# Attention roots, rotations and query splits with an operand in PSUM, keys rotated ahead of their root, and a minimum collected with its sign

## The chip, the cores and the metric

The kernel runs on one core of a Trainium2 chip. Its time is device time in microseconds (us) of one execution; three executions of the kernel before took 2225.22, 2225.4 and 2231.34 us. The engines are TensorE (PE, with its weight loads shown apart as PEld), VectorE (DVE), ScalarE (ACT), GpSimd (POOL) and SyncE (SP), which issues the transfers. [...]

## The reference

Four layers run over 256 latent tokens with a prefix of 256 context tokens, each layer followed by a gated MLP. Layers 0 and 3 are windowed attention with sink logits (16 query heads and 4 key heads of 64), layer 1 is multi-head latent attention (MLA), layer 2 a gated recurrence. What the change touches is the root of each head's norm, the rotation and the softmax:

```python
def rmsnorm(x, gain):
    xf = x.astype(jnp.float32)
    y = xf * lax.rsqrt(jnp.mean(xf * xf, axis=-1, keepdims=True) + EPS)
    return (y * gain.astype(jnp.float32)).astype(x.dtype)

def attend(q, k, v, mask=None, sink=None):
    s = jnp.einsum("bqhgd,bkhd->bhgqk", q, k, preferred_element_type=jnp.float32) * (q.shape[-1] ** -0.5)
    ...
    m = jnp.max(s, axis=-1)
    ...
        m = jnp.maximum(m, sk)
    p = jnp.exp(s - m[..., None])
    denom = jnp.sum(p, axis=-1)
```

Queries and keys are normalised per head (`rmsnorm`), then latent ones are rotated: each half of a head is multiplied with cosines, and its swapped copy with sines is added. A norm's factor is one number for each token and head, so it commutes with the rotation. MLA does the same on heads of 96, of which 32 are rotated, and norms two low-rank projections besides.

## The kernel before

The 512 tokens lie in four blocks b of 128 (0 and 1 context, 2 and 3 latent). Every weight is used as a sum of two halves for precision: SP loads `raw`, ACT rounds it to `whi` (L222), POOL subtracts to get `wlo` (L226, in pieces of 128x256), and each product is three matmuls (L235, L236, L237). A framework places every engine's instructions in one static order, and reorders attention work around the projections. PSUM has four pools of two banks each (128x512): mm, fl, mo and tp. A bank is free for its next product once its last reader is done.

An inverse root has no instruction of its own on this path: `mean_rsqrt` and `rsqrt` (L272 to L287) work it out on DVE from an integer shift, a magic constant and three Newton steps, 12 instructions on tiles of 128x4, 128x8 or 128x16, all of them in SBUF (`rs_v`, `rs_i`, `rs_y`, `rs_t`):

```python
for _ in range(steps):
    nc.vector.tensor_tensor(t, y, y, op=ALU.mult)
    nc.vector.scalar_tensor_tensor(t, t, -0.5, v, op0=ALU.mult, op1=ALU.mult)
    nc.vector.scalar_tensor_tensor(y, t, 1.5, y, op0=ALU.add, op1=ALU.mult)
```

There are 30 such roots: 24 on 128x8 (12 for queries of the windowed layers, 12 in MLA's loop), 4 on 128x16 and 2 on 128x4. The layers' own norms have another, `psum_rsqrt` (L289 to L300), in which each instruction has an operand in PSUM; it runs 15 times.

Windowed attention (`swa`, L576 on) goes as follows. *Keys*, L634 to L658: ACT copies a block of the keys out of PSUM (`kraw`, L638), copies the values, squares `kraw` (L641); DVE sums by head (L642). After the fourth block one root of 128x16 follows, then for each block a multiply by it (L650), the rotation (L617, or L574, L621 and L622 for latent blocks), ACT's doubling copy (L655), and PE's transposes (L660), which are split into `k_hi` and `k_lo` (L269, L270). *Queries*, `q_post`, L663 to L691: ACT squares the PSUM bank, DVE sums (L674) and rotates into `qr` in SBUF; each half is split (ACT L681, DVE L682), transposed (L685) and copied; the root becomes `rqs`, a factor of the scores (L691). *Cores*, L699 to L755: the scores (L696, L697), for latent blocks one instruction that scales, masks and takes the maximum (L723), a sign change (L726), the exponential (L727), the division, transposes (L745) and the product with the values (L751). Products of the next head group, `proj(2)`, go into the fl banks between them. Layer 3 handles latent queries only.

MLA (`mla`, L783 on) runs in head groups. For each block of the next group `kv_mm` makes keys and values, `q_mm` makes queries in an fl bank (L899 to L913, rotation in L908 and L909), one root of 128x8 serves both, then `kv_put` multiplies the keys by it (L883, L884, into `kn`) and transposes them (L888), and `q_scale` (L920) makes `rqs`.

## Time and profile before

| | before |
|---|---|
| runs (us) | 2225.4, 2231.34, 2225.22 |
| profiled execution: its own time | 2225.85 us |
| its span | 2224.0 us |
| PE busy, share of the span | 2122.6 us, 95% |
| DVE busy | 1549.0 us, 70% |
| ACT busy | 1037.4 us, 47% |
| POOL busy | 1050.3 us, 47% |
| mean granted clock | 0.983 |

The span runs from the first to the last instruction; 1.85 us lie around it. Busy shares are averages over stages with different limits. The chain of waits is followed back from the last instruction. A timeline row gives start, duration, engine, line, output and inputs, shape and count, and in brackets the idle time before it and what released it. Matmuls are pipelined, so their durations overlap.

### The profile page before, as it was taken

The page shows a single profiled execution, that of the slowest core. Times are in us where ns is not written, and L with a number is a line of the kernel's source. Part 1 is how long each engine was busy: PE and PEld are TensorE (multiplying, and loading weights), DVE is VectorE, ACT ScalarE, POOL GpSimd, SP SyncE. Part 2 cuts the span into 40 slices and gives each one's busy share as a digit, 9 for nine tenths or more (in the row PEclk, how much of TensorE's full clock was granted, in tenths as well). Part 3 has the DMA queues.
Part 4 walks back from the last instruction along what each step waited for, and adds up shares of the span by engine and source line. Part 5 has one row for each costly group of instructions (what it writes and reads, how often), then busy time and mean ns, then how long its engine had stood idle before and what let it go on. Part 6 is the DMA issues. An engine that isn't in the chain of part 4 may idle for free.

```text
span 2224.0 us, 32888 instructions
## 1 busy us (share of the span) xinstructions
PE 2122.6 (95%) x12084; PEld 1764.6 (79%) x12084; DVE 1549.0 (70%) x3341; ACT 1037.4 (47%) x1860; POOL 1050.3 (47%) x760
## 2 busy tenths in 40 slices
PE   6999999999999999999999999889999999898999
PEld 4666888888888666878888887678888888678999
DVE  4677779777776886687888677857954456785333
ACT  4467553232346775532233376824332324675544
POOL 3331255544544113455455457654544444526887
PEclk9999999999999999999999999999999999999999
DMA  7534145554532011255555422224655552313665
GB/s 300 199 127 131 39 135 179 172 178 157 180 114 68 21 30 55 60 190 178 174 186 181 132 67 87 94 88 131 194 184 163 177 163 86 105 33 114 187 182 160
DMA packets 83888, 300.14 MB, mean 135 GB/s; under 512 B 11152, under 2 KB 12816, under 8 KB 81296
## 3 DMA queue, kind: packets, MB, share of 16 engines
q1 hardware_dynamic: 83728, 298.05, 41.9%
q8 instruction: 95, 1.56, 0.3%
q14 instruction: 65, 0.53, 0.1%
HBM read 296.97 MB, written 1.05 MB: 134 GB/s over the span
## 4 chain that ended last, share of the span: by engine, by line
PE 78%; DVE 13%; ACT 4%; DMA 2%; issue 1%; POOL 1%; SPq 0%; ACTq 0%; DVEq 0%
PE fl L235 8%; PE fl L236 8%; PE fl L237 8%; PE mm L236 7%; PE mm L237 7%; PE mm L235 7%; PE mo L235 4%; PE mo L236 4%; PE mo L237 4%; PE tp L235 3%; PE tp L236 3%; PE tp L237 3%; PE mo L751 2%; PE mm L938 2%; PE tp L745 2%
## 5 line engine op out<-in xcount | busy, mean ns | idle before, releaser
L226 POOL TENSOR_TENSOR wlo<-raw,whi 128x256 fp32r<-128x256 f32 (+3 forms) x709 | 1015.6, 1455 | 1106.4 <-ACT whi L222 1068.9
L222 ACT ACTIVATE whi<-raw 128x1024 fp32r<-128x1024 f32 (+3 forms) x367 | 382.5, 1043 | 493.0 <-PE tp L236 208.0
L397 DVE SCALAR_TENSOR_TENSOR junk<-mw,cbc 128x1024 bf16<-128x1024 f32 x256 | 463.8, 1812 | 28.6 <-DMA mw<-in_modw_dram 15.0
L237 PE MATMUL fl<-h_hi,wlo 128*128 128x512 f32 (+1 forms) x800 | 287.1, 359 | 0.1
L235 PE MATMUL fl<-h_hi,whi 128*128 128x512 f32 (+1 forms) x800 | 286.7, 358 | 0.0
L236 PE MATMUL fl<-h_lo,whi 128*128 128x512 f32 (+1 forms) x800 | 286.3, 358 | 0.0
L236 PE MATMUL mm<-h_lo,whi 128*128 128x512 f32 (+1 forms) x784 | 274.6, 352 | 2.5 <-POOL h_lo L463 1.1
L235 PE MATMUL mm<-h_hi,whi 128*128 128x512 f32 (+1 forms) x784 | 273.3, 350 | 2.5 <-ACT h_hi L459 2.5
L237 PE MATMUL mm<-h_hi,wlo 128*128 128x512 f32 (+1 forms) x784 | 273.1, 349 | 0.0
L1193 DVE SCALAR_TENSOR_TENSOR conv<-mm,colt,conv 128x510 f32<-128x510 f32 (+1 forms) x88 | 59.8, 679 | 188.9 <-ACT conv L1191 188.9
L1197 ACT ACTIVATE conv<-conv 128x512 f32<-128x512 f32 (+1 forms) x88 | 51.0, 580 | 291.1 <-DVE conv L1195 291.0
L237 PEld LDWEIGHTS fl<-h_hi,wlo 128*128 128x128 f32 x800 | 151.3, 189 | 23.2 <-POOL wlo L226 1.4
L236 PEld LDWEIGHTS fl<-h_lo,whi 128*128 128x128 f32 x800 | 151.3, 189 | 21.7
L235 PEld LDWEIGHTS fl<-h_hi,whi 128*128 128x128 f32 x800 | 151.5, 189 | 21.5
L236 PEld LDWEIGHTS mm<-h_lo,whi 128*128 128x128 f32 x784 | 148.2, 189 | 24.6 <-DVE h_lo L465 2.9
L235 PEld LDWEIGHTS mm<-h_hi,whi 128*128 128x128 f32 x784 | 148.6, 190 | 22.2 <-ACT h_hi L459 3.5
L237 PEld LDWEIGHTS mm<-h_hi,wlo 128*128 128x128 f32 x784 | 148.3, 189 | 18.8
L235 PE MATMUL mo<-g_hi,whi 128*128 128x512 f32 (+1 forms) x388 | 135.0, 348 | 8.3 <-DVE x L471 8.2
L471 DVE SCALAR_TENSOR_TENSOR x<-mo,modc,x 128x256 f32<-128x256 f32 x193 | 86.5, 476 | 76.5 <-PE mo L237 76.4
L237 PE MATMUL mo<-g_hi,wlo 128*128 128x512 f32 (+1 forms) x388 | 134.8, 347 | 0.0
L236 PE MATMUL mo<-g_lo,whi 128*128 128x512 f32 (+1 forms) x388 | 134.7, 347 | 0.0
L235 PE MATMUL tp<-g_hi,whi 128*128 128x512 f32 (+1 forms) x352 | 124.7, 354 | 0.0
(356 smaller groups left out, 4452.8 us busy)
## 6 DMA issues: line engine op xcount, KB each, us to landing
raw<-in_W_dram SPq DMA_DIRECT2D x352, 512.0 KB, 3.6
mw<-in_modw_dram SPq DMA_DIRECT2D x144, 512.0 KB, 4.2
mw<-in_modwa_dram SPq DMA_DIRECT2D x8, 1024.0 KB, 16.0
mw<-in_modwb_dram SPq DMA_DIRECT2D x16, 512.0 KB, 4.5
mw<-in_modwb_dram SPq DMA_DIRECT2D x8, 1024.0 KB, 9.4
cbc<-in_cc_dram SPq DMA_DIRECT2D x3, 1024.0 KB, 6.7
raw<-in_W_dram SPq DMA_DIRECT2D x8, 384.0 KB, 3.1
x<-in_xT_dram SPq DMA_DIRECT2D x8, 256.0 KB, 4.1
```

The lines of the kernel that those rows point to most:

```text
L222: nc.scalar.activation(hi, raw, AF.Copy)
L226: nc.gpsimd.tensor_tensor(lo[:, cs], raw[:, cs], f32(hi[:, cs]), op=ALU.subtract)
L235: nc.tensor.matmul(ps, ah, bh, start=start and i == 0, stop=False, **kw)
L236: nc.tensor.matmul(ps, ah, bl, start=False, stop=False, **kw)
L237: op = nc.tensor.matmul(ps, al, bh, start=False, stop=stop and i == n - 1, **kw)
L397: nc.vector.scalar_tensor_tensor(junk, raw, 1.0, cbc[:, s], op0=ALU.mult, op1=ALU.mult, accum_out=modc[l][:, s, m:m + 1])
L471: nc.vector.scalar_tensor_tensor(X[m][:, half], ps[:, half], modc[l][:, s, part + m:part + m + 1], X[m][:, half], op0=ALU.mult, op1=ALU.add)
L745: nc.tensor.transpose(pp[:, c:c + 128], P[z][:, (2 * kp + kk) * 128:(2 * kp + kk + 1) * 128], ident)
L751: nc.tensor.matmul(po[r], v[0][:, kb, p * 128 + 64 * z:p * 128 + 64 * z + 64], pt[:, kp, (kk * 2 + z) * 128:(kk * 2 + z + 1) * 128], start ...
L938: nc.tensor.matmul(ps[:, c], d["q"][:96, 2 * hp + z, bc], d["k"][:96, 2 * hp + z, :nk], start=True, stop=True)
L1193: op = nc.vector.scalar_tensor_tensor(y3[:, :, 1:], g3[:, :, :255], cw[:, l, 0, f:f + 1], y3[:, :, 1:], op0=ALU.mult, op1=ALU.add)
L1197: nc.scalar.activation(y[:, t0:], y[:, t0:], AF.Silu)
```

## The change

1. `psum_rsqrt` takes the room to work in: its `v` and `t` lie in PSUM, `y` in SBUF, and it has 12 instructions instead of 13. It is now used for 29 of the 30 roots that were all in SBUF; MLA's first root of 128x16 for keys keeps the old form. The room is the bank of the product itself (`pkv[3]`, the query's `ps`, or columns 384 on of MLA's bank).
2. Keys: ACT squares straight from PSUM, the copy `kraw` is gone, DVE rotates straight from the PSUM bank ahead of the root (for latent blocks one product is written back into PSUM), and the multiply by the root follows (L650, now on the rotated keys).
3. Queries: the rotation stays in the PSUM bank, the split reads it there, and the root comes after the split.
4. The latent cores' L723 takes a minimum on scores of the opposite sign (`rqs` is negated for latent blocks) and collects it where the sign change put its result; L726 is gone, and the exponential scales by -1.
5. MLA's query rotation of latent blocks: two instructions become three, two of which have an operand in PSUM on the way into `qn`.

```diff
-    def psum_rsqrt(ps, n, dim):
-        src, v2, i, y = (ps[:, a * n:(a + 1) * n] for a in range(4))
-        v, t, r = small(n, "rs_v"), small(n, "rs_t"), small(n, "rs_y")
-        nc.vector.tensor_scalar(v2, src, 1.0 / dim, EPS, op0=ALU.mult, op1=ALU.add)
-        nc.vector.tensor_scalar(i.bitcast(I32), v2.bitcast(I32), 1, None, op0=ALU.logical_shift_right)
-        nc.vector.tensor_scalar(y.bitcast(I32), i.bitcast(I32), -1.0, MAGIC, op0=ALU.mult, op1=ALU.add)
+    def psum_rsqrt(room, src, n, dim):
+        v, t, y = room[:, :n], room[:, n:2 * n], small(n, "rs_y")
         nc.vector.tensor_scalar(v, src, 1.0 / dim, EPS, op0=ALU.mult, op1=ALU.add)
-        for z in range(3):
-            nc.vector.tensor_tensor(t, y, v, op=ALU.mult)
+        nc.vector.tensor_scalar(t.bitcast(I32), v.bitcast(I32), 1, None, op0=ALU.logical_shift_right)
+        nc.vector.tensor_scalar(y.bitcast(I32), t.bitcast(I32), -1.0, MAGIC, op0=ALU.mult, op1=ALU.add)
+        for _ in range(3):
+            nc.vector.tensor_tensor(t, v, y, op=ALU.mult)
             nc.vector.scalar_tensor_tensor(t, t, -0.5, y, op0=ALU.mult, op1=ALU.mult)
-            nc.vector.scalar_tensor_tensor(r if z == 2 else y, t, 1.5, y, op0=ALU.add, op1=ALU.mult)
-        return r
+            nc.vector.scalar_tensor_tensor(y, t, 1.5, y, op0=ALU.add, op1=ALU.mult)
+        return y
 
...
             rope_swap(r.rearrange("p (h d) -> p h d", d=64), s3, sg[:, b - 2:b - 1], nh)
-            nc.vector.tensor_tensor(d3, s3, cg[:, b - 2:b - 1].to_broadcast([128, nh, 64]), op=ALU.mult)
-            nc.vector.tensor_tensor(dst, dst, r, op=ALU.add)
+            nc.vector.tensor_tensor(s3, s3, cg[:, b - 2:b - 1].to_broadcast([128, nh, 64]), op=ALU.mult)
+            nc.vector.tensor_tensor(dst, src, r, op=ALU.add)
...
         ssk = small(16, "ssk")
-        kraw = [tmp("kraw"), tmp("kraw")]
+        kr2 = [tmp("kr"), tmp("kr")]
         for b in range(4):
             ps = pkv[b]
-            kb = kraw[b // 2][:, (b % 2) * 256:(b % 2 + 1) * 256]
-            nc.scalar.activation(kb, ps[:, :256], AF.Copy)
+            sq = tmp("sq")[:, :256]
+            nc.scalar.activation(sq, ps[:, :256], AF.Square)
             put(sel(v, slice(None), b), ps[:, 256:])
-            sq = tmp("sq")[:, :256]
-            nc.scalar.activation(sq, kb, AF.Square)
             nc.vector.tensor_reduce(ssk[:, b * 4:(b + 1) * 4], sq.rearrange("p (h d) -> p h d", d=64), axis=AX.X, op=ALU.add)
-        rk = mean_rsqrt(ssk, 16, 64)
+            rotate(kr2[b // 2][:, (b % 2) * 256:(b % 2 + 1) * 256], ps[:, :256], b, 4, gk, cgk, sgk)
+        rk = psum_rsqrt(pkv[3], ssk, 16, 64)
...
         for b in range(4):
-            kb = kraw[b // 2][:, (b % 2) * 256:(b % 2 + 1) * 256]
-            k3 = kb.rearrange("p (h d) -> p h d", d=64)
+            kr = kr2[b // 2][:, (b % 2) * 256:(b % 2 + 1) * 256]
+            k3 = kr.rearrange("p (h d) -> p h d", d=64)
             nc.vector.tensor_tensor(k3, k3, rk[:, b * 4:(b + 1) * 4].rearrange("p (h o) -> p h o", o=1).to_broadcast([128, 4, 64]),
                                     op=ALU.mult)
-            kr = tmp("kr")[:, :256]
-            rotate(kr, kb, b, 4, gk, cgk, sgk)
             krs.append(probs())
...
-            qr = tmp("qr")
-            rotate(qr, ps, b, 8, gq, cgq, sgq)
+            rotate(ps, ps, b, 8, gq, cgq, sgq)
...
-                q4 = qr[:, z * 256:(z + 1) * 256].rearrange("p (h d) -> p h d", h=4)
+                q4 = ps[:, z * 256:(z + 1) * 256].rearrange("p (h d) -> p h d", h=4)
...
                     nc.vector.tensor_copy(qb[:, z], pq)
-            rq = mean_rsqrt(ss, 8, 64)
-            nc.vector.tensor_scalar(rqs[p][:, b * 8:(b + 1) * 8], rq, 0.125, None, op0=ALU.mult)
+            rq = psum_rsqrt(ps, ss, 8, 64)
+            nc.vector.tensor_scalar(rqs[p][:, b * 8:(b + 1) * 8], rq, 0.125 if b < 2 else -0.125, None, op0=ALU.mult)
...
                     nc.vector.tensor_tensor_reduce(
-                        out=pt, in0=ps, in1=mask[:, b - 2], op0=ALU.add, op1=ALU.max,
-                        scale=rq2[:, z:z + 1], scalar=sk[:, z:z + 1], accum_out=mx[:, z:z + 1])
-                    nc.vector.tensor_scalar(ngm[:, z:z + 1], mx[:, z:z + 1], -1.0, None, op0=ALU.mult)
-                    nc.scalar.activation(pt, pt, AF.Exp, bias=ngm[:, z:z + 1], accum_out=den[:, z:z + 1])
+                        out=pt, in0=ps, in1=mask[:, b - 2], op0=ALU.add, op1=ALU.min,
+                        scale=rq2[:, z:z + 1], scalar=nsk2[:, z:z + 1], accum_out=ngm[:, z:z + 1])
+                    nc.scalar.activation(pt, pt, AF.Exp, bias=ngm[:, z:z + 1], scale=-1.0, accum_out=den[:, z:z + 1])
...
             bc = slice(b * 128, (b + 1) * 128)
-            ps = (mm_ps() if hg == 0 and b % 2 else fl_ps())[:, :384]
+            full = mm_ps() if hg == 0 and b % 2 else fl_ps()
+            ps = full[:, :384]
...
-                nc.vector.tensor_tensor(qn, p3, cgq[:, b - 2:b - 1].to_broadcast([128, 4, 96]), op=ALU.mult)
-                nc.vector.tensor_tensor(qn[:, :, 64:], qn[:, :, 64:], r, op=ALU.add)
+                cb = cgq[:, b - 2:b - 1]
+                nc.vector.tensor_tensor(qn[:, :, :64], p3[:, :, :64], cb[:, :, :64].to_broadcast([128, 4, 64]), op=ALU.mult)
+                nc.vector.tensor_tensor(p3[:, :, 64:], p3[:, :, 64:], cb[:, :, 64:].to_broadcast([128, 4, 32]), op=ALU.mult)
+                nc.vector.tensor_tensor(qn[:, :, 64:], p3[:, :, 64:], r, op=ALU.add)
...
+            return full[:, 384:]
...
-                    q_mm(hg + 1, b, ss[:, 4:8])
-                    rr = mean_rsqrt(ss, 8, 96)
+                    room = q_mm(hg + 1, b, ss[:, 4:8])
+                    rr = psum_rsqrt(room, ss, 8, 96)
```

DVE around the key root of layer 3, in the order of the kernel before (`ssk` the sums, `rs_*` the root, `kraw` the keys, `kr` the rotated keys):

```order
L642 TENSOR_REDUCE ssk<-sq 128x4 x4
L286 TENSOR_SCALAR rs_v<-ssk 128x16
...
L281 SCALAR_TENSOR_TENSOR rs_y<-rs_t,rs_y 128x16
L650 TENSOR_TENSOR kraw<-kraw,rs_y 128x256 x2
L617 TENSOR_TENSOR kr<-kraw,rowt 128x256 x2
L650 TENSOR_TENSOR kraw<-kraw,rs_y 128x256 x2
L574 TENSOR_TENSOR rot<-kraw,sks 128x256
L621 TENSOR_TENSOR kr<-kraw,skc 128x256
```

And in the changed kernel, whose line numbers are lower by 2 to 8 here:

```order
L638 TENSOR_REDUCE ssk<-sq 128x4
L615 TENSOR_TENSOR kr<-mm,rowt 128x256
L638 TENSOR_REDUCE ssk<-sq 128x4
L615 TENSOR_TENSOR kr<-mm,rowt 128x256
L638 TENSOR_REDUCE ssk<-sq 128x4
L572 TENSOR_TENSOR rot<-fl,sks 128x256
L619 TENSOR_TENSOR fl<-fl,skc 128x256
L620 TENSOR_TENSOR kr<-fl,rot 128x256
L638 TENSOR_REDUCE ssk<-sq 128x4
...
L297 SCALAR_TENSOR_TENSOR rs_y<-fl,rs_y 128x16
L647 TENSOR_TENSOR kr<-kr,rs_y 128x256 x4
```

The rotations have moved from behind the root to between the sums, and only the four multiplies stand behind it.

PE at the first key transposes of layer 3 before (`mm<-whi,h_hi` is the query projection, `P` the doubled keys):

```order
L237 MATMUL mm<-whi,h_lo 128x512
L660 MATMUL tp<-tabt,P 128x128 x2
L235 MATMUL mm<-whi,h_hi 128x512
L660 MATMUL tp<-tabt,P 128x128 x2
L236 MATMUL mm<-wlo,h_hi 128x512
```

And in the changed kernel:

```order
L236 MATMUL mm<-wlo,h_hi 128x512
L655 MATMUL tp<-tabt,P 128x128 x2
L237 MATMUL mm<-whi,h_lo 128x512
L655 MATMUL tp<-tabt,P 128x128 x2
L235 MATMUL mm<-whi,h_hi 128x512
L236 MATMUL mm<-wlo,h_hi 128x512
```

Of that projection's matmuls 24 stood behind the first transposes before, and 16 do now: 8 have moved ahead of them.

PE in layer 0, from the second scores of the first core to the first product of `proj(2)`, before (L363 are small products for the modulation of later layers, L685 the query transposes):

```order
L697 MATMUL mm<-k_lo,q 128x256
L363 MATMUL mo<-mw_790,condT 32x512 x3
L696 MATMUL mm<-k_hi,q 128x256
L685 MATMUL tp<-tabt,qhl 128x128 x8
L697 MATMUL mm<-k_lo,q 128x256
L696 MATMUL mm<-k_hi,q 128x256
L697 MATMUL mm<-k_lo,q 128x256
L363 MATMUL mo<-mw_792,condT 32x512 x4
L363 MATMUL mo<-mw_832,condT 32x512 x4
L363 MATMUL mo<-mw_871,condT 32x512
L235 MATMUL fl<-whi,h_hi 128x512
```

And the rows up to the same product in the changed kernel:

```order
L738 MATMUL tp<-tabt,P 128x128 x4
L679 MATMUL tp<-tabt,qhl 128x128 x4
L744 MATMUL mo<-pt,v 64x128 x4
L679 MATMUL tp<-tabt,qhl 128x128 x4
L690 MATMUL mm<-k_hi,q 128x256
L691 MATMUL mm<-k_lo,q 128x256
L690 MATMUL mm<-k_hi,q 128x256
L691 MATMUL mm<-k_lo,q 128x256
L361 MATMUL mo<-mw_1003,condT 32x512
L738 MATMUL tp<-tabt,P 128x128 x4
L679 MATMUL tp<-tabt,qhl 128x128 x4
L235 MATMUL fl<-whi,h_hi 128x512
```

The first product of `proj(2)` has moved behind the transposes (now L738) of two cores.

## Rows read from the trace of the kernel before

**Rows 1.** The page: busy time, share and instructions; the chain that ended last.
```profile
PE 2122.6 (95%) x12084; PEld 1764.6 (79%) x12084; DVE 1549.0 (70%) x3341; ACT 1037.4 (47%) x1860; POOL 1050.3 (47%) x760
...
PE 78%; DVE 13%; ACT 4%; DMA 2%; issue 1%; POOL 1%; SPq 0%; ACTq 0%; DVEq 0%
```

**Rows 2.** Timeline of DVE, layer 3's keys: start, us, engine, line, operation.
```profile
1899.83 0.42 DVE L642 TENSOR_REDUCE ssk<-sq 128x4 f32<-128x256 f32 x1 [0.94 <-ACT sq L641]
...
1900.91 0.68 DVE L279 TENSOR_TENSOR rs_t<-rs_y 128x16 f32<-128x16 f32 x1
...
1906.45 0.17 DVE L281 SCALAR_TENSOR_TENSOR rs_y<-rs_t,rs_y 128x16 f32<-128x16 f32 x1
1906.66 0.76 DVE L650 TENSOR_TENSOR kraw<-kraw,rs_y 128x256 f32<-128x256 f32 x2
```

**Rows 3.** Timeline of POOL in the same stretch.
```profile
1900.83 5.56 POOL L226 TENSOR_TENSOR wlo<-raw,whi 128x256 fp32r<-128x256 f32 x8 [2.91 <-ACT whi L222]
```

**Rows 4.** Timeline, a norm's root in PSUM on DVE, and POOL meanwhile.
```profile
1882.00 0.16 DVE L298 SCALAR_TENSOR_TENSOR rs_t<-rs_t,tp 128x2 f32<-128x2 f32 x1
...
1881.29 1.58 POOL L463 TENSOR_TENSOR h_lo<-hw,h_hi 128x256 fp32r<-128x256 f32 x2 [0.97 <-ACT hw L462]
```

**Rows 5.** All of one line's instructions: count, ns min/median/max, starts, forms.
```profile
L279 DVE TENSOR_TENSOR rs_t<-rs_y x90: 146/166/737, 64.6 to 1971.5; 128x8 f32<-128x8 f32 x72, 128x16 f32<-128x16 f32 x12, 128x4 f32<-128x4 f32 x6
...
L297 DVE TENSOR_TENSOR rs_t<-tp,rs_v x45: 145/158/160, 15.9 to 2025.9; 128x2 f32<-128x2 f32 x45
```

**Rows 6.** DVE's groups by line: count, busy us, mean ns, idle before.
```profile
L281 DVE SCALAR_TENSOR_TENSOR rs_y<-rs_t,rs_y 128x8 f32<-128x8 f32 (+2 forms) x90 | 22.5, 250 | 1.4
...
L279 DVE TENSOR_TENSOR rs_t<-rs_y 128x8 f32<-128x8 f32 (+2 forms) x90 | 21.6, 240 | 1.7
...
L726 DVE TENSOR_SCALAR st<-st 128x1 f32<-128x1 f32 x64 | 8.3, 145 | 0.1
```

**Rows 7.** Timeline of PE, layer 3: first key transposes, first query transposes.
```profile
1908.47 0.69 PE L660 MATMUL tp<-tabt,P 128*128 128x128 f32 x2 [4.23 <-ACT P L655]
...
1923.70 0.63 PE L685 MATMUL tp<-tabt,qhl 128*128 128x128 f32 x4 [1.95 <-DVE qhl L682]
```

**Rows 8.** Stretches: us, busy of PE, PEld, DVE, ACT, POOL; clock, DMA, GB/s.
```profile
95.00:265.00 170.00, 162.71 (x1175) 111.82 (x1175) 131.02 (x484) 115.04 (x302) 38.21 (x53) 1.00 0.32 105
1904.00:1908.00 4.00, 0.23 (x2) 0.00 (x0) 3.83 (x9) 0.21 (x1) 2.39 (x4) 0.81 0.64 164
1908.00:1912.00 4.00, 3.53 (x11) 2.87 (x12) 3.28 (x9) 3.15 (x5) 2.04 (x3) 0.50 0.26 100
844.00:848.00 4.00, 3.02 (x10) 2.55 (x11) 1.87 (x6) 1.93 (x4) 0.69 (x1) 0.62 0.61 200
801.00:803.00 2.00, 2.00 (x9) 1.55 (x8) 1.93 (x6) 0.00 (x0) 1.29 (x3) 0.50 0.54 217
1925.00:2003.00 78.00, 71.57 (x551) 55.16 (x550) 70.06 (x256) 56.56 (x138) 18.52 (x27) 0.98 0.17 53
```

**Rows 9.** Timeline of PE and DVE at MLA's key transposes.
```profile
844.98 1.06 PE L888 MATMUL tp<-tabt,kn 128*96 128x128 f32 x4 [3.75 <-DVE rqs L920]
...
799.15 0.62 PE L888 MATMUL tp<-tabt,kn 128*96 128x128 f32 x4 [2.08 <-DVE rqs L920]
...
754.60 0.61 PE L888 MATMUL tp<-tabt,kn 128*96 128x128 f32 x4 [2.12 <-DVE kn L884]
...
841.15 0.65 DVE L279 TENSOR_TENSOR rs_t<-rs_y 128x8 f32<-128x8 f32 x1
...
843.20 0.91 DVE L883 TENSOR_TENSOR kn<-kraw,rs_y 128x256 f32<-128x256 f32 x1
```

**Rows 10.** Timeline of PE, layer 0: key transposes, first product of `proj(2)`.
```profile
70.35 0.69 PE L660 MATMUL tp<-tabt,P 128*128 128x128 f32 x2 [2.46 <-ACT P L655]
...
101.34 0.47 PE L235 MATMUL fl<-whi,h_hi 128*128 128x512 f32 x1 [0.30 <-DVE st L729]
```

**Rows 11.** PE's waits: what it waited for, us in total, times, longest.
```profile
PE tp L448 <- DVE rs_y L299: 6.8, 7, 2.6
```

More of the change, by code (lines that the diff above doesn't have):

```diff
@@ L444, in rsq @@
                     nc.tensor.matmul(ps[:, b:b + 1], a[:, b * 128:(b + 1) * 128], ones, start=z == 0, stop=z == 1)
-            rs = psum_rsqrt(ps, 2, D)
+            rs = psum_rsqrt(ps[:, 2:], ps[:, 0:2], 2, D)
             rb = ps[:, 256:]
@@ L801, in mla @@
         for c, w, ks in ((0, 288, (3, 3, 2)), (1, 384, (2, 2, 2, 2))):
-            ps = [(mm_ps() if b < 2 else fl_ps())[:, :w] for b in range(4)]
+            full = [mm_ps() if b < 2 else fl_ps() for b in range(4)]
+            ps = [p[:, :w] for p in full]
             def part(bs, q):
@@ L839, in mla @@
                     nc.scalar.activation(sq[:, :32], dn[:, b, 256:288], AF.Square, accum_out=ssr[:, b:b + 1])
-            nc.vector.tensor_copy(rrs[c], mean_rsqrt(ss, 4, (256, 384)[c]))
+            nc.vector.tensor_copy(rrs[c], psum_rsqrt(full[3][:, 384:], ss, 4, (256, 384)[c]))
             if c == 1:
@@ L976, in mla @@
         for b in range(4):
-            q_mm(0, b, ss[:, b * 4:(b + 1) * 4])
-        q_scale(0, 0, 4, mean_rsqrt(ss, 16, 96))
+            room = q_mm(0, b, ss[:, b * 4:(b + 1) * 4])
+        q_scale(0, 0, 4, psum_rsqrt(room, ss, 16, 96))
         units = {}
```

## The prediction, made before the changed kernel had run

> **What bounds the kernel now.** I read the page first. PE is busy 95% of the span and makes up 78% of the chain that ended last, DVE 13% [rows 1]. So nearly all of the kernel is bound by matmuls that the change leaves alone, and what can be won lies in the few places where PE stands still behind DVE, in the clock behind them, and in stretches where DVE is nearly as full as PE. PE's timeline, searched for long waits in attention, shows those places: 4.23 us at the first key transposes of layer 3 and 1.95 at its first query transposes [rows 7], 3.75, 2.08 and 2.12 at three key transposes of MLA [rows 9], 2.46 at those of layer 0 [rows 10]. Behind each stands the end of a root or what hangs on it. [...] And while layer 3's cores run, DVE is busy 70.06 of 78 us and PE 71.57, so neither alone is the bound; in layer 0's cores DVE has 131 of 170 and PE 162.7 [rows 8].
>
> **Why the roots are slow there.** In layer 3 the last sum ends at 1900.25 and the first multiply by the root starts at 1906.66: 6.4 us for 12 tiny instructions. They take 0.68 us each, until one at 1906.45 takes 0.17 [rows 2]. POOL runs its subtractions from 1900.83 to 1906.39 [rows 3]: exactly as long. Over the kernel the first of the three Newton instructions takes 0.146 to 0.737 us [rows 5], and mean 0.240 to 0.250 [rows 6]. A norm's root, whose instructions have an operand in PSUM, takes 0.16 in the middle of a POOL subtraction [rows 4], and the slowest of 45 took 0.160 [rows 5]. So an SBUF-only root next to POOL costs four times its price, and one with an operand in PSUM does not wait. [...]
>
> **The change part by part.** Terms are against the profiled execution's own 2225.85 us; the median of the three runs is 0.45 lower.
>
> *Layer 3's keys: 6.2 gained.* The root falls from 6.4 us to 12 instructions of 0.16 with gaps of 0.04, 2.4 us. The rotations move ahead of it, into the idle time of 0.94 us that DVE has before each sum [rows 2]; only the last block's, some 1.2 us (three instructions at 0.4, an estimate from the multiply's 0.76 for two), stays on the path between sum and root, where the rotation of the first block stood behind the root before. ACT's key copies ahead of the squares are gone. The path from last sum to transposes thus shortens by some 4 us, and the query projection's 8 matmuls that moved ahead of the transposes cover more. The 4.23 us goes, and so does the half clock behind it: 4 us at 0.50 lost 2.0.
>
> *Layer 3's first queries: 1.9.* The wait of 1.95 [rows 7] is for the split, whose DVE part reads two SBUF operands next to POOL, behind a root that shares DVE with it. Now it reads PSUM and the root comes after it. I take all but the rounding; bounds 0 and 1.95.
>
> *Layer 3's cores: 3.5.* 32 of the 64 L726 lie here, 32 x 0.145 = 4.6 us of DVE [rows 6]; three query roots save 36 x (0.24 - 0.16) = 2.9. If DVE were the bound, 7.5; if PE, nothing. DVE has 8 us of idle time and PE 6.4 [rows 8], so I take the middle, 3.5 (0 to 7.5).
>
> *MLA: 9.5.* The three waits add up to 7.95. At 841.15 the root's instructions take 0.65 [rows 9], so eight of them save some 4, which is more than any one wait. The clock of 0.62 from 844 to 848 and of 0.50 from 801 to 803 lost 1.5 and 1.0 [rows 8]. That is 10.45. Against it stand the multiplies behind the root, L883 and L884, which still have two SBUF operands (0.91 [rows 9]), and a bank that is held longer: the query's fl bank was free after the rotation, and is now kept until the root has ended, some 12 x 0.2 = 2.4 us later, twelve times. PE has the next keys' six matmuls and the cores' scores to do meanwhile. I subtract 1 for both (0 to 12, below). The three-instruction rotation costs about 1 us of DVE in all, off the path.
>
> *Layer 0's keys: 2.* The wait of 2.46 [rows 10]; POOL is less busy there and ACT now converts a weight ahead of the last square, so I leave the clock behind it out. Bounds 0 and 4.
>
> *Layer 0's lead into the cores: -3.* Here the change makes something later. Query banks were free after the rotation; now also after split and root, some 4 us later (two splits on ACT and DVE, 12 x 0.2, `rqs`). The first product of `proj(2)` needs the first fl bank; before, it waited 0.30 us [rows 10]. In the new order it stands behind two cores' transposes, so that PE has less to fill the cores' start with. Queued behind it on PE is everything, and DVE's own queue has the later queries' rotations behind the root. One wait of about 4, mostly covered by small products: 3 (0 to 8, one wait for each fl bank).
>
> *Layer 0's cores: 1.5.* As in layer 3, 4.6 us of L726 and the roots, but PE is at 162.7 of 170 and DVE at 131 [rows 8]; 0 to 5.
>
> *Norms: 1.2.* One instruction less, and seven of the roots end a wait of PE [rows 11]: 7 x 0.17.
>
> Sum: 6.2 + 1.9 + 3.5 + 9.5 + 2 - 3 + 1.5 + 1.2 = 22.8 us. 2225.85 - 22.8 = 2203.05; less 0.45, 2203.
>
> [...] The slowest norm root instruction with an operand in PSUM took 0.160 us, where the median of SBUF's is 0.166 [rows 5], so PSUM costs no more here even without POOL. If it did, the roots' gain in quiet stretches would turn into a loss. [...]
>
> **The rivals.**
> *Only the waits go (half the gain).* The four places lose their waits, 4.23 + 1.95 + 7.95 + 2.46 = 16.6, less 3 for layer 0's lead; but the clock falls anyway, at the next small wait, and PE rather than DVE bounds the cores. 2225.85 - 13.6 = 2212. For it: the clock also falls at waits of 2 us (0.50 from 801 to 803). A dearer PSUM instruction would end here too. Chance 0.23, 2209 to 2217.
> *More than that.* Both sets of cores are DVE-bound and the lead costs nothing: 4 + 3.5 + 3 more, 2192. Against it: PE at 95%. 0.10.
> *Nothing to measure.* The change speeds up the roots, but what is late next takes their place: L650 and L883 still have two SBUF operands, ACT's copy and the splits follow, and the transposes wait for those. Then each wait shrinks by a quarter, about 4 us: 2222. 0.10.
> *Slower: banks held until the root's end.* Each query bank, of which fl has two, is now held through split and root. If PE comes to the bank before, it stands: 8 us in layer 0 (two fl banks), 12 in MLA (12 x 1.0, the 2.4 less what six matmuls cover), 4 in layer 3: 24, and with the clock behind the waits (2.0 for 4.23 above, so x 1.5) 36. The gains without the lead's -3 are 25.8, so 2225.85 - 25.8 + 36 = 2236. It decides once such waits exceed 25.8 / 1.5 = 17 us. Against it: PE has other work between two uses of a bank, and `proj(2)` had only 0.30 us of waiting [rows 10]. 0.07.
>
> **How the numbers follow.** The forecast, 2203 (2196 to 2209), has 0.50. The range runs from 2194 to 2219: it takes in the forecast's bounds and the half gain, and leaves out most of the larger gain, the unchanged and the slower case, some 0.2. A measurement can tell 0.3%, 6.7 us, from no change, so faster means under 2218.7: 0.50 + 0.23 + 0.10 = 0.83. Same 0.10, slower 0.07.
>
> **What would show it.** The key root of layer 3 at 0.16 us an instruction while POOL subtracts; no wait over 1 us at the first key transposes of layer 3 and MLA; a granted clock near 1.00 around 1908 and 844; DVE's busy time lower by some 30 us. I am wrong if the new instructions take 0.6 or more next to POOL, if the waits reappear at the same transposes behind L650 or L883, or if PE waits for DVE at the first products into fl and mm banks.

## The result

The changed kernel takes 2246.28 us (median of 4 runs, 2244.19 to 2248.08) against 2225.75 for the kernel before: 1.0081 times as long, 95% interval 1.0066 to 1.0095. It is 0.8% slower. Ratios here and below are given with their intervals; they are not the plain quotient of two medians, which would be 1.0092 here. Forecast were 2203, with 2194 to 2219 as range. The profiled execution has a span of 2246.3 us, 22.3 more than before.

The page of the changed kernel, busy time and share of the span, and the engines of the chain that ended last, to be read against [rows 1]:

```profile
PE 2130.2 (95%) x12084; PEld 1762.6 (78%) x12084; DVE 1516.7 (68%) x3270; ACT 1036.1 (46%) x1852; POOL 1045.3 (47%) x760
...
PE 78%; DVE 11%; ACT 4%; DMA 3%; issue 2%; POOL 1%; SPq 0%; ACTq 0%; DVEq 0%
```

DVE has 71 instructions and 32 us of work less, as the change intends. PE has as many matmuls, is busy 8 us longer, and stands still for 116 us instead of 101. To see where, I cut both traces at the same matmuls: first query transposes of layer 0, last product with the values there, first key transposes and last product of MLA's loop, the first matmul with the root of the norm ahead of layer 3, and layer 3's first query transposes and last product (differences of start times in the two timelines).

| stage | before | after | |
|---|---|---|---|
| start to first query transposes, layer 0 | 93.1 | 90.2 | -2.9 |
| layer 0, to the last product with the values | 165.2 | 181.6 | +16.4 |
| to MLA's first key transposes | 446.6 | 445.8 | -0.8 |
| MLA's loop, to its last product | 187.2 | 202.4 | +15.2 |
| to the norm ahead of layer 3 | 979.6 | 976.6 | -3.0 |
| to layer 3's first query transposes | 52.0 | 45.7 | -6.3 |
| layer 3's cores, to the last product | 86.0 | 91.0 | +5.0 |
| rest | 214.3 | 213.0 | -1.3 |

So the stretches ahead of the cores are faster, as forecast, and the cores themselves lose 36.6 us. The granted clock is the share of its full speed that the trace records for TensorE; the traces of before and after hold 1.00 and 0.50 alone, and a figure between them is a mean over its stretch. Three stretches of the changed kernel (us, then busy us and instructions of PE, PEld, DVE, ACT and POOL, granted clock, DMA share, GB/s), the cores of layer 0, MLA's loop and layer 3's cores:

```profile
90.00:272.00 182.00, 163.09 (x1132) 108.38 (x1132) 122.70 (x460) 113.55 (x299) 33.70 (x48) 0.94 0.29 95
...
717.00:920.00 203.00, 180.88 (x1095) 127.97 (x1095) 141.40 (x518) 128.29 (x306) 33.21 (x50) 0.95 0.11 35
...
1942.00:2033.00 91.00, 80.65 (x612) 60.43 (x611) 72.58 (x243) 63.02 (x149) 22.07 (x32) 0.96 0.18 53
```

The same three of the kernel before:

```profile
93.00:258.00 165.00, 157.71 (x1144) 106.90 (x1142) 130.54 (x488) 113.92 (x298) 38.02 (x52) 1.00 0.33 109
...
705.00:892.00 187.00, 174.60 (x1095) 126.33 (x1095) 145.38 (x508) 127.49 (x306) 33.27 (x50) 0.97 0.13 37
...
1924.00:2010.00 86.00, 79.19 (x622) 61.48 (x621) 75.13 (x269) 61.46 (x147) 22.51 (x32) 0.98 0.18 53
```

In layer 0 PE's idle time (length less busy) rises from 7.3 to 18.9 us and the clock falls from 1.00 to 0.94, and PE's busy time rises by 5 us for nearly as many matmuls; in MLA idle time rises from 12.4 to 22.1 and PE's busy time by 6. DVE has less to do in both, so what shows is PE waiting and the clock behind that, not more work on DVE. PE's waits there, MLA's loop first (engine, tile and line, what it waited for, us in all, times, longest):

```profile
PE fl L235 <- DVE rs_y L297: 6.5, 6, 1.9
PE tp L909 <- DVE qn L906: 4.8, 4, 1.6
PE tp L882 <- DVE kn L878: 2.9, 2, 2.3
PE fl L235 <- ACT v L865: 2.7, 1, 2.7
PE fl L235 <- ACT kraw L867: 2.7, 1, 2.7
PE mm L936 <- DVE rs_y L297: 2.5, 1, 2.5
...
PE tp L882 <- DVE rqs L918: 0.5, 2, 0.3
```

the same loop before:

```profile
PE tp L888 <- DVE rqs L920: 5.8, 2, 3.8
PE tp L888 <- DVE kn L884: 4.4, 2, 2.3
PE tp L888 <- DVE st L949: 1.6, 2, 1.4
PE fl L235 <- DVE qn L904: 1.3, 1, 1.3
```

layer 0's cores in the changed kernel:

```profile
PE mm L690 <- ACT P L710: 8.7, 3, 4.3
PE mo L361 <- DMA mw<-in_modwb_dram: 6.7, 3, 4.4
PE mm L690 <- DVE st L717: 2.2, 4, 0.7
```

and before:

```profile
PE tp L745 <- DVE P L737: 3.3, 2, 2.2
PE mo L363 <- DMA mw<-in_modwb_dram: 2.8, 4, 1.0
```

The first line of all is new: the first product into an fl bank waits for L297, the last instruction of a root. The timeline of DVE and of PE at one such place of the changed kernel:

```profile
816.71 0.29 DVE L906 TENSOR_TENSOR qn<-fl,sq 128x128 f32<-128x128 f32 x1
...
819.30 0.17 DVE L297 SCALAR_TENSOR_TENSOR rs_y<-fl,rs_y 128x8 f32<-128x8 f32 x1
...
819.61 0.41 PE L235 MATMUL fl<-whi,cq_hi 128*128 128x384 f32 x1 [1.85 <-DVE rs_y L297]
```

PE has nothing to do for 1.85 us, until a root of another block has left the bank that the next query product needs. The rotation's last instruction (L906) had ended at 817.00 and the root ends at 819.47, so the bank is held 2.5 us longer. In layer 0 the waits have another face, at scores behind an exponential, because what used to stand between the scores is gone; there the waits for the modulation's weights (`mw`) are longer too, 6.7 us instead of 2.8, which no run takes apart. PE's timeline of the changed kernel, a late score and the first product of `proj(2)`, and the root of block 2's queries on DVE:

```profile
108.35 0.58 PE L690 MATMUL mm<-k_hi,q 128*128 128x256 f32 x1 [4.29 <-ACT P L710]
...
112.88 0.48 PE L235 MATMUL fl<-whi,h_hi 128*128 128x512 f32 x1
...
109.04 0.16 DVE L297 SCALAR_TENSOR_TENSOR rs_y<-fl,rs_y 128x8 f32<-128x8 f32 x1
```

That product ran at 101.34 before [rows 10] and now stands at 112.88, behind two cores. It does not wait there: the root in block 2's bank had ended at 109.20. The hold acts here through the place in PE's order.

### The profile page after: what moved, and what is told of

Same layout as the page of the kernel before. It is cut to its first block, busy times and chain, and to the rows that moved or that the text cites. A ratio compares the mean times of both kernels' runs of the same rounds, so it can differ in the third digit from the quotient of the medians.

```text
span 2246.3 us, 32823 instructions
## 1 busy us (share of the span) xinstructions
PE 2130.2 (95%) x12084; PEld 1762.6 (78%) x12084; DVE 1516.7 (68%) x3270; ACT 1036.1 (46%) x1852; POOL 1045.3 (47%) x760
## 4 chain that ended last, share of the span: by engine, by line
PE 78%; DVE 11%; ACT 4%; DMA 3%; issue 2%; POOL 1%; SPq 0%; ACTq 0%; DVEq 0%
PE fl L235 9%; PE fl L236 9%; PE fl L237 9%; PE mm L236 7%; PE mm L237 7%; PE mm L235 7%; PE mo L235 4%; PE mo L236 4%; PE mo L237 4%; PE tp L235 3%; PE tp L236 3%; PE tp L237 3%; PE mo L744 2%; PE mm L936 2%; PE tp L738 2%
## 5 line engine op out<-in xcount | busy, mean ns | idle before, releaser
L226 POOL TENSOR_TENSOR wlo<-raw,whi 128x256 fp32r<-128x256 f32 (+3 forms) x709 | 1011.1, 1448 | 1139.4 <-ACT whi L222 1063.6
L395 DVE SCALAR_TENSOR_TENSOR junk<-mw,cbc 128x1024 bf16<-128x1024 f32 x256 | 462.2, 1805 | 30.3 <-DMA mw<-in_modw_dram 18.2
L1191 DVE SCALAR_TENSOR_TENSOR conv<-mm,colt,conv 128x510 f32<-128x510 f32 (+1 forms) x88 | 59.8, 679 | 187.0 <-ACT conv L1189 186.9
L235 PEld LDWEIGHTS fl<-h_hi,whi 128*128 128x128 f32 x800 | 151.9, 190 | 21.5
```

Of the source, the lines that this page charges most:

```text
L226: nc.gpsimd.tensor_tensor(lo[:, cs], raw[:, cs], f32(hi[:, cs]), op=ALU.subtract)
L235: nc.tensor.matmul(ps, ah, bh, start=start and i == 0, stop=False, **kw)
L395: nc.vector.scalar_tensor_tensor(junk, raw, 1.0, cbc[:, s], op0=ALU.mult, op1=ALU.mult, accum_out=modc[l][:, s, m:m + 1])
L1191: op = nc.vector.scalar_tensor_tensor(y3[:, :, 1:], g3[:, :, :255], cw[:, l, 0, f:f + 1], y3[:, :, 1:], op0=ALU.mult, op1=ALU.add)
```

## Experiments

Two theories. **Held bank**: a query bank is now taken until its root has ended, so the next product into it comes later, by a wait or by its place in the order. **Dearer work**: the new instructions, or the longer chain in one bank, cost the time themselves. Times are compared by the ratio to runs of the kernel before on the same chip, where its median was 2227.8 to 2230.6. Every edit below is against the kernel named. Stage times are of one profiled execution each, and stages with the same code differ by up to 4 us between kernels.

**Taking parts back.** From the changed kernel, queries of the windowed layers:

```diff
-            rotate(ps, ps, b, 8, gq, cgq, sgq)
+            qr = tmp("qr")
+            rotate(qr, ps, b, 8, gq, cgq, sgq)
...
-            rq = psum_rsqrt(ps, ss, 8, 64)
+            rq = mean_rsqrt(ss, 8, 64)
```

with the split reading `qr` and the old rotation into it.

> The changed kernel (2246 us) with only the windowed layers' queries put back: rotated into SBUF, split from there, their 12 roots all in SBUF. Keys, minimum and MLA stay as changed. Theory of the held bank (the cores of layers 0 and 3 lost 16.4 and 5.0 us because query banks stay taken until their root ends, so that the next projection stands later in PE's order): both come back, 2225, and the first product of the next projection in layer 0 starts before 103 us instead of at 112.9. Rival, a dearer core (the new minimum or exponential is what costs time in the cores): stays near 2246.

Measured 2233.94, ratio 1.0024 (1.0011 to 1.0036). Layer 0's cores took 166.2 us and the first product of `proj(2)` stood at 101.06: all of the loss there is gone, as it is in layer 3's cores (86.0). MLA's loop took 206.6. The total is 9 above the expected one. In the profiled execution (2239.81; the ten lie between 2226.72 and 2239.81) MLA took 4 us more than in the changed kernel and the lead of layer 0 2 more; why stays open. MLA as before instead:

```diff
-                    rr = psum_rsqrt(room, ss, 8, 96)
+                    rr = mean_rsqrt(ss, 8, 96)
```

with the roots of 16 and 4 columns and the rotation put back too:

> The changed kernel with MLA as before: its roots of 8, 16 and 4 columns in SBUF and its two-instruction rotation; the windowed layers stay as changed. Held bank: MLA's loop lost 15.2 us, most of it where PE waits for the root's last instruction at the first product into an fl bank (6 waits, 6.5 us) and at the scores (2.5): 2231. Rival, that MLA only inherits a worse order and would lose as much without the PSUM roots: 2246.

Measured 2231.31, 1.0016 (1.0004 to 1.0028). MLA's loop 186.7, layer 0's cores 184.5. As expected. Both edits in one kernel:

> Both put back: only the keys of the windowed layers, their root in PSUM, the minimum collected with its sign and the norms' shorter root are new. Held bank: the two losses are separate places and add up, 2246 - 21 - 15 = 2210, some 15 us faster than the kernel before (the lead of layer 3 gained 6 in the changed kernel). Rival, that the losses are one thing which moves (what is won in one place waits in the next): 2225 or more.

Measured 2213.99, 0.9938 (0.9920 to 0.9956): the losses add up, and a kernel 0.6% faster than the one before is left. This "reduced kernel" (keys, minimum and norm root new) is the base of what follows. Its cores took 166.5, 185.5 and 85.0 us.

**The root's hold, against rotation and split.** From the changed kernel, only the windowed queries' root in SBUF:

```diff
-            rq = psum_rsqrt(ps, ss, 8, 64)
+            rq = mean_rsqrt(ss, 8, 64)
```

> The changed kernel with one thing put back: the 12 query roots of the windowed layers work in SBUF, while rotation and split stay in the query's PSUM bank. If the root holds the bank too long, the loss in layers 0 and 3 goes as with all of the query part put back: 2225. If the rotation and split in PSUM hold it (they come ahead of the root), it stays: 2240 to 2246.

Measured 2228.77, 1.0008 (0.9998 to 1.0018). Layer 0's cores 172.8: putting the root back takes 9 of 16, and rotation and split in PSUM keep the rest. Layer 3 was faster than in any run so far, 97.0 us from first key transposes to last product (before: 101.2). In MLA, from the reduced kernel, the roots alone in the product's bank (those of 16 and 4 columns too), and then the rotation alone:

```diff
-                    rr = mean_rsqrt(ss, 8, 96)
+                    rr = psum_rsqrt(room, ss, 8, 96)
```

> The kernel with queries and MLA put back (2214), with one thing of MLA changed: the 12 roots of its loop, the one of 16 and those of 4 columns work in the product's own bank. Rotation as before. Held bank: the 15 us of MLA come with this alone, 2227 to 2230, and PE waits for a root's last instruction at first products into fl. If the three-instruction rotation causes them (4.8 us of waits at the query transposes): 2214.

Measured 2229.45, 0.9997 (0.9987 to 1.0008), loop 201.8, as expected.

```diff
-                nc.vector.tensor_tensor(qn, p3, cgq[:, b - 2:b - 1].to_broadcast([128, 4, 96]), op=ALU.mult)
-                nc.vector.tensor_tensor(qn[:, :, 64:], qn[:, :, 64:], r, op=ALU.add)
+                cb = cgq[:, b - 2:b - 1]
+                nc.vector.tensor_tensor(qn[:, :, :64], p3[:, :, :64], cb[:, :, :64].to_broadcast([128, 4, 64]), op=ALU.mult)
+                nc.vector.tensor_tensor(p3[:, :, 64:], p3[:, :, 64:], cb[:, :, 64:].to_broadcast([128, 4, 32]), op=ALU.mult)
+                nc.vector.tensor_tensor(qn[:, :, 64:], p3[:, :, 64:], r, op=ALU.add)
```

> The other half of MLA's part alone: the rotation in three instructions, all roots of MLA in SBUF, queries put back. Held bank: the rotation ends only some 0.3 us later and holds the bank no longer than that, 2212 to 2217. If the rotation is the cause: 2225 or more.

Measured 2214.97, 0.9933 (0.9917 to 0.9950), loop 186.9. So MLA's whole loss comes with the roots in the query's bank; the 4.8 us of waits behind the three-instruction rotation do not count without them.

**The hold without the root in PSUM.** This separates the two theories. Reduced kernel, all roots in SBUF, one tiny write into the query's bank after each:

```diff
                     rr = mean_rsqrt(ss, 8, 96)
+                    nc.vector.tensor_copy(room[:, :8], rr)
```

> The kernel with queries and MLA put back (2214): every root of MLA's loop in SBUF, but after each root one copy of 128x8 writes its result into the query's bank, which is thus held until the root has ended, as with the root in PSUM; twelve copies cost DVE some 2 us themselves. If holding the bank is the cause: MLA's loop from first key transposes to last product takes some 200 us instead of 186, 2227 to 2232 in all. If the root's instructions with an operand in PSUM are what costs: 2213 to 2217.

Measured 2229.42, 0.9994 (0.9979 to 1.0008), loop 200.8. The stretch of this kernel, and PE's longest waits in it (the copy is L992):

```profile
699.00:900.00 201.00, 179.96 (x1107) 128.49 (x1109) 143.77 (x520) 128.61 (x306) 32.80 (x50) 0.95 0.11 34
```

```profile
PE fl L235 <- ACT kraw L869: 5.7, 2, 2.8
PE fl L235 <- DVE fl L992: 5.1, 5, 1.9
PE tp L912 <- DVE qn L909: 4.4, 3, 1.6
```

The twelve copies by themselves (count, busy us, mean ns, idle before):

```profile
L992 DVE COPY fl<-rs_y 128x8 f32<-128x8 f32 x12 | 2.0, 169 | 0.4
```

Length, PE's idle time (21.0) and clock are those of the changed kernel, with no root in PSUM. Over all kernels here MLA's loop, counted to the end of its last product, took 201.2 to 207.5 us in the five that hold the query's bank until the root's end, and 186.4 to 189.5 in the eleven that hold no bank for it. The roots lie in SBUF here, where their Newton instructions (L279 to L281) took 0.209 to 0.233 us in the mean over the kernel, against 0.162 to 0.170 in the fl banks of the changed one (L295 to L297); nine times the difference, an estimate, makes the hold some 0.5 us longer than there. A copy into SBUF, as a control, was not run, but the twelve copies are 2.0 us of DVE's work against 15 us. In MLA the held bank is shown to be the cause. It acts through PE's order as well as by waits: of the loop's 1111 matmuls 166 stand elsewhere than in the reduced kernel, and the runs do not take the two apart. The same for the windowed queries:

```diff
             rq = mean_rsqrt(ss, 8, 64)
+            nc.vector.tensor_copy(ps[:, :8], rq)
```

> The kernel with queries and MLA put back (2214), in which each of the 12 query roots of the windowed layers, all in SBUF as before, is followed by one copy of 128x8 into the query's bank, so that this bank is held until the root has ended while rotation, split and root work as before. If the hold alone makes layer 0's loss: its cores take 176 us or more from first query transposes to last product instead of 166.6, and the first product of the next projection starts after 108 us; 2224 to 2232 in all. If the split from PSUM or the roots' instructions there are needed for it: 2213 to 2217.

Measured 2219.59, 0.9956 (0.9942 to 0.9969). Layer 0's cores 173.6, the first product of `proj(2)` at 103.82: on all three less than for a hold that does it all, and more than for no effect. The hold alone makes 7 of layer 0's 16 us. With the root itself in the bank, rotation and split in SBUF:

```diff
-            rq = mean_rsqrt(ss, 8, 64)
+            rq = psum_rsqrt(ps, ss, 8, 64)
```

> The kernel with queries and MLA put back (2214), in which the 12 query roots alone work in the query's bank; rotation and split stay in SBUF. Layer 0's cores took 166.6 us with none of it in PSUM, 172.8 with rotation and split there, 173.6 with the bank only held until the root's end, 184.5 with all of it (MLA as before). If the two add up, the root alone gives some 174 to 178 us, 2220 to 2226 in all. If the loss needs the split ahead of the root in the same bank: 167 to 169, 2214.

Measured 2218.29, 0.9946 (0.9925 to 0.9966), layer 0's cores 176.2. Over the reduced kernel that is 9.7; rotation and split gave 6.3; together 16.0, and the kernel with all of it took 15 (changed kernel) and 18 (MLA put back). So in the profiled executions they add up, which rests on one execution each: the four of this kernel took 2214.1, 2214.33, 2222.26 and 2222.71, and the profiled one is the last. The profiled one is 9.7 over the reduced kernel's (2213.03), with layer 3's lead 3 us shorter and MLA's loop 3 longer. The first product of `proj(2)` tells the same: it starts 8.5 us behind the first query transposes in the reduced kernel, 12.7 with rotation and split in the bank, 15.0 with the hold alone, 16.9 with the root alone and 22.7 with all of it, in the order of the cores' times. That rotation and split lose by the bank and not by their own price is argued: the three instructions of a latent rotation take at most 0.02 us more each (medians 0.686, 0.700 and 0.692 us against 0.681, 0.680 and 0.682 before), and ACT's part of the split takes less (0.378 against 0.406); no run holds the bank for them alone.

**A bank of its own.** If only the query's bank must not be held, the root may use another:

```diff
-            rq = mean_rsqrt(ss, 8, 64)
+            rq = psum_rsqrt(mo_ps(), ss, 8, 64)
...
-                    rr = mean_rsqrt(ss, 8, 96)
+                    rr = psum_rsqrt(mo_ps(), ss, 8, 96)
```

> The kernel with queries and MLA put back (2214), in which the 12 query roots and the 12 roots of MLA's loop again have an operand in PSUM, but in a bank of their own from the mo pool instead of the query's bank. If only holding the query's bank was wrong, the cores keep their time (layer 0's from first query transposes to last product 166 us, MLA's 186) and the waits at MLA's key transposes (13.1 us) fall by half or more: 2200 to 2207. If a PSUM bank held through a root costs wherever it is (the mo banks serve the cores' output and the modulation), it is slower than 2214.

Measured 2219.16, 0.9949 (0.9931 to 0.9966): no faster than the reduced kernel, perhaps slower. Layer 0 kept its time (167.8), but MLA's loop took 196.4. 11 of the 15 us are lost here too. The mo banks serve the cores' output; that holding them is the reason is argued, since no run holds them without the root, and the tp and mm pools were not tried.

**The small parts.** The reduced kernel with the old keys, then two parts alone on the kernel before:

```diff
-        rk = psum_rsqrt(pkv[3], ssk, 16, 64)
+        rk = mean_rsqrt(ssk, 16, 64)
...
+            rotate(kr, kb, b, 4, gk, cgk, sgk)
```

> The kernel with queries and MLA put back (2214), with the keys put back too: only the minimum with its sign and the norms' shorter root remain. By the prediction's terms the keys carry 4.23 + 2.0 in layer 3 and 2 in layer 0, so 2222; the wait of some 4 us at layer 3's first key transposes is back. If instead the minimum in the cores carries the gain: 2214 to 2216.

Measured 2218.54, 0.9948 (0.9933 to 0.9963). The wait of 4.2 us at the key transposes is back, and the lead of layer 0 is 6.4 us longer, that of layer 3 3.3; but other stages were faster by 4, and the two intervals overlap. So the keys' gain is shown in its place and only in part in the total. The norms' root alone (the new `psum_rsqrt` with this call):

```diff
-            rs = psum_rsqrt(ps, 2, D)
+            rs = psum_rsqrt(ps[:, 2:], ps[:, 0:2], 2, D)
```

> The kernel before with the norms' shorter root alone. By the prediction's term for it, 7 x 0.17 = 1.2 us faster than before. With keys, queries and MLA all put back, the minimum and this root together were 0.5% faster than before; if the root carries most of that, 6 or more.

Measured 2220.88, 0.9949 (0.9933 to 0.9964). One tiny instruction less in 15 roots makes the kernel 0.5% faster (9 us by the medians, 11 by the ratio), some eight to nine times the price I gave it. The minimum alone:

```diff
-                        out=pt, in0=ps, in1=mask[:, b - 2], op0=ALU.add, op1=ALU.max,
+                        out=pt, in0=ps, in1=mask[:, b - 2], op0=ALU.add, op1=ALU.min,
```

with its sign, and L726 gone.

> The kernel before with the minimum collected with its sign alone, 64 sign changes less. By the prediction's terms (part of 3.5 and of 1.5) some 3 us faster than before. By the difference of the two runs above (norm root and minimum 0.5%, norm root alone 0.5%): no change.

Measured 2231.06, 1.0009 (0.9997 to 1.0020): nothing.

One place where the norm root's gain shows is a gated MLP. The same 10 us of both kernels, first the kernel before:

```profile
320.00:330.00 10.00, 7.17 (x32) 5.62 (x31) 9.66 (x16) 3.24 (x4) 4.91 (x2) 0.98 0.61 196
```

```profile
328.75 0.47 PE L235 MATMUL mo<-g_hi,whi 128*128 128x512 f32 x1 [2.83 <-DVE x L471]
```

```profile
314.77 1.23 DVE L397 SCALAR_TENSOR_TENSOR junk<-mw,cbc 128x1024 bf16<-128x1024 f32 x1 [3.02 <-ACT cbc L1224]
...
316.04 3.47 DVE L397 SCALAR_TENSOR_TENSOR junk<-mw,cbc 128x1024 bf16<-128x1024 f32 x1
...
324.07 3.13 DVE L397 SCALAR_TENSOR_TENSOR junk<-mw,cbc 128x1024 bf16<-128x1024 f32 x1 [0.34 <-DMA mw<-in_modw_dram]
...
316.03 2.39 POOL L226 TENSOR_TENSOR wlo<-raw,whi 128x1024 fp32r<-128x1024 f32 x1 [3.04 <-ACT whi L222]
323.73 2.39 POOL L226 TENSOR_TENSOR wlo<-raw,whi 128x1024 fp32r<-128x1024 f32 x1 [5.31 <-ACT whi L222]
```

then with the shorter norm root:

```profile
320.00:330.00 10.00, 8.54 (x38) 6.77 (x37) 8.89 (x18) 3.24 (x4) 4.79 (x2) 1.00 0.60 209
```

```profile
327.52 0.47 PE L235 MATMUL mo<-g_hi,whi 128*128 128x512 f32 x1 [1.46 <-DVE x L469]
...
317.55 2.53 DVE L395 SCALAR_TENSOR_TENSOR junk<-mw,cbc 128x1024 bf16<-128x1024 f32 x1
...
323.60 2.38 DVE L395 SCALAR_TENSOR_TENSOR junk<-mw,cbc 128x1024 bf16<-128x1024 f32 x1 [1.11 <-DMA mw<-in_modw_dram]
```

The rows of L226 are POOL's. DVE's long products for the modulation (L397, all operands in SBUF), 1.23 us at 314.77, took 3.47 and 3.13 where POOL subtracted at the same time, and PE waited 2.83 us behind them. With the shorter norm root the slow ones (L395 there) took 2.53 and 2.38, and PE waited 1.46. That is 1.4 of some 10 us. That a shift against POOL's work is why, and that the other gated MLPs gain in the same way, is argued from these rows; no run shows it by itself. The framework's order is a rival: 118 of PE's 12084 matmuls stand elsewhere in this kernel, all of them next to norms.

**A faster version.** Layer 3 alone rotates and splits in PSUM, root in SBUF:

```diff
-            qr = tmp("qr")
+            qr = ps if q0 else tmp("qr")
```

> The kernel with queries and MLA put back (2214), in which layer 3 alone rotates and splits its queries in their PSUM bank, with the root in SBUF. With that in both layers, layer 3 took 97.0 us from first key transposes to last product and layer 0's cores 172.8; without it 99.9 and 166.6. If it pays where few queries wait for banks: 2211. If the 3 us were chance: 2214.

Measured 2209.36, 0.9896 (0.9880 to 0.9912), layer 3 97.7 us from first key transposes to last product: the fastest, 1% under the kernel before and 1.8% under the changed one. Against the reduced kernel (0.9938, 5 to 9 us more) layer 3 accounts for some 2. Counted to the end of the last product it takes 98.1 us here and 100.7 in the reduced kernel, but 98.9 in the kernel with the hold in MLA, whose layer 3 is the reduced kernel's. So it is not shown that layer 3's split is what gains. With layer 3's roots in mo banks besides:

```diff
-            rq = mean_rsqrt(ss, 8, 64)
+            rq = psum_rsqrt(mo_ps(), ss, 8, 64) if q0 else mean_rsqrt(ss, 8, 64)
```

> The fastest so far (2209: queries of layer 3 rotated and split in PSUM, their root in SBUF, MLA and layer 0's queries put back), with the four roots of layer 3's queries in a bank of their own from the mo pool. Query lead and cores of layer 3 took 97.7 us there; with roots in their own bank but the old split, 98.3. If the root is what is late at the first scores: 2 us faster, 2207. If the mo bank is missed by the cores: 2210 or more.

Measured 2211.69, 0.9913 (0.9897 to 0.9928), layer 3 97.2: no gain.

## Why the prediction was wrong, step by step

*The roots' price: right.* The changed kernel's timeline at layer 3's key root, DVE, POOL and PE:

```profile
1926.73 0.18 DVE L291 TENSOR_SCALAR fl<-ssk 128x16 f32<-128x16 f32 x1
...
1929.09 0.17 DVE L297 SCALAR_TENSOR_TENSOR rs_y<-fl,rs_y 128x16 f32<-128x16 f32 x1
1929.29 3.34 DVE L647 TENSOR_TENSOR kr<-kr,rs_y 128x256 f32<-128x256 f32 x4
...
1924.80 9.12 POOL L226 TENSOR_TENSOR wlo<-raw,whi 128x256 fp32r<-128x256 f32 x12 [2.10 <-ACT whi L222]
...
1930.73 0.44 PE L655 MATMUL tp<-tabt,P 128*128 128x128 f32 x2
...
1942.29 0.63 PE L679 MATMUL tp<-tabt,qhl 128*128 128x128 f32 x4
```

The root takes 2.5 us in the middle of POOL's subtractions, where it took 6.4 [rows 2], and the first key and query transposes wait for nothing [rows 7]; from 1928 to 1932 the clock was 1.00, where it had been 0.50 [rows 8]. The prediction's "0.68 us each" was right for eight of the twelve; the first three, ahead of POOL's start, took 0.17 to 0.18. The first Newton instruction of the new roots, in fl banks:

```profile
L295 DVE TENSOR_TENSOR fl<-fl,rs_y x72: 154/170/182, 68.3 to 1992.0; 128x8 f32<-128x8 f32 x60, 128x16 f32<-128x16 f32 x6, 128x4 f32<-128x4 f32 x6
```

The slowest takes 0.182 us where 0.737 was the slowest before [rows 5], and the median is 0.170 against 0.166: 0.004 us more with an operand in PSUM. What spares such an instruction the wait beside POOL is not shown.

*Layer 3's lead, 6.2 + 1.9: right in sum, partly by luck.* 6.3 gained of 8.1, and both waits are gone. But with the queries put back the lead takes 49.0 us instead of 52.0, so keys and norm root together gave 3.0 where 6.2 was forecast for the keys, and the queries 3.3 where it was 1.9. Nor was it the split that gained for the queries: with rotation and split in PSUM and the root in SBUF the lead was only 0.7 shorter than that, with the root alone there 3.0. *Layer 0's keys, 2:* 2.9 gained.

*MLA, 9.5: wrong, the step that failed.* The waits at the key transposes fell as forecast, from 11.8 us in all to 3.4, though one of 2.3 us is left, over the 1 us that the prediction named as a sign. But "I subtract 1 for both (0 to 12)" for the bank held longer was the wrong end of its own bounds. The length of the hold, 2.4 us, was right (2.5 in the row above); what it costs was not. The loop lost 15.2, and with the 9.5 not had that is 25 us off. I took it that PE had six matmuls and scores to do meanwhile. In the kernel's code two fl banks alternate between keys and queries, and the rows show the next query product at the head of PE's queue, waiting for DVE. This is the last sign of being wrong that the prediction named: PE waits for DVE at first products into fl (6.5 us) and mm banks (2.5).

*Layer 0's lead into the cores, -3, and cores, 1.5: wrong.* The loss was 16.4, past the bound of 8. I had read in the new order that `proj(2)` starts two cores later and priced it as one wait at one bank. It meant that scores, exponentials and transposes of two cores ran with nothing between them: idle time of 18.9 us instead of 7.3, and a clock of 0.94 instead of 1.00. Of the 11.6 us more, 3.9 are at the modulation's weights.

*Layer 3's cores, 3.5: wrong sign.* 5.0 lost with rotation, split and root in one bank. With rotation and split there and the root in SBUF the cores took 82.8 us, with the root alone there 84.9, against 86.0 before and 85.0 in the reduced kernel. The nine kernels with the old queries lie within 3 us, so neither is shown to gain in the cores; only all of it together loses.

*Norms, 1.2: far too small*, 0.5% (9 to 11 us) alone. *The minimum:* nothing, so the 64 sign changes were not on the path, and the middle between "DVE is the bound" and "PE is" was no price for them.

The right case was the last rival, banks held until the root's end; its cause is what the runs show. That it priced the losses at 36 us and the three places lost 36.6 is chance: the 36 were to be set against gains, of which 14.5 us were forecast in the same places (9.5, 1.5 and 3.5), so its net loss there was 21.5. It came to 2236, 10 us short. It got 0.07, because one row (0.30 us of waiting at one product [rows 10]) was read as room to spare. That row told of the order of the kernel before, in which the bank came free just in time. DVE there:

```profile
100.52 0.68 DVE L621 TENSOR_TENSOR qr<-fl,sqc 128x512 f32<-128x512 f32 x1
```

The last reader of the bank ends at 101.20 and the product starts at 101.34; a bank that is just in time has no slack.

## What to carry to other kernels

Before putting a step's operands in PSUM, ask until when the bank is then taken and which product comes into it next: a bank that is filled again 0.14 us after its last reader has no slack for 2.4 us more, and the cost is the wait, the slower clock behind it (0.94 and 0.95 here), and the work that the order moves away. Take a change of several parts apart: here one part (the norm root) was worth 0.5%, one nothing, two cost 15 us or more each, and the good ones together made a kernel 1% faster. A tiny write into a bank, placed where the new last reader would stand, measures a hold before the work is moved.

## What the runs showed that I had not expected

Twelve copies of 128x8 into held banks, 0.169 us each, cost 12 to 15 us (0.9994 against 0.9938). One instruction less in 15 norm roots gave 0.5%. And a root in a bank of another pool (mo) was no way out: MLA's loop still lost 11 us.
